# All cache pages by plain transfers of the SP queue, weight requests moved to ACT, no transfers on POOL

## The chip, the cores and the metric

The kernel runs on one core of one Trainium2 chip. The metric is the device time of one execution in microseconds; lower is better. The engines are named as the profile names them: PE is TensorE's matmuls, PEld its weight loads, DVE is VectorE, ACT is ScalarE, POOL is GpSimd and SP is SyncE. Each engine runs its own list of instructions in order. SP, ACT and POOL can also request DMA transfers; a request is an instruction in the list of the engine that makes it.

## The reference

Two layers of a decoder trunk run over 288 tokens: a prompt of 256 and 8 samples of 4 tokens each. Each layer is a half-step feed-forward block, a mixer and a second half-step feed-forward block:

```python
x = x + 0.5 * _swiglu(_rmsnorm(x, g_ffn1), w_up1, w_down1)
u, v, q, k, vv, qi, ki, wi, ga, gb = split(_rmsnorm(x, g_mix) @ w_in)
sv, attn = mixer(...)            # chunked spatial gating; sparse attention
x = x + (sigmoid(ga) * ((gelu(u) * sv) @ w_pa) + sigmoid(gb) * (attn @ w_pb)) @ w_out
x = x + 0.5 * _swiglu(_rmsnorm(x, g_ffn2), w_up2, w_down2)
# sample mixer: a paged cache of 2048 past positions for each of 8 samples
ki_all = concatenate([cache_kidx[page_table], ki])   # 16 pages of 128 positions a sample
_, idx = top_k(index_scores(qi, wi, ki_all), 256)
attn = sparse_attend(q, cache_k[phys, off], cache_v[phys, off], valid)
```

Model width is 1024, feed-forward width 2816, 8 heads of 128, 2 key heads. The page table is data: which page of the pool holds which positions is known only at run time. The kernel scores all keys and masks those outside the top 256, so each layer reads all 128 pages of the index cache, of the key cache and of the value cache.

## The kernel before, in words

All work on weights is a list of 420 units. A unit is a block of 128 output columns of a weight matrix, 128 x 8 x 128 numbers (512 KB; 448 KB in the second and third third of a down-projection). `unit_dma(i)` requests unit i from memory into one of four buffers `raw`. `unit_split(i)` cuts it into a high and a low part: ACT copies `wh` from `raw`, then DVE subtracts `wl` from `raw` and `wh`; each of the two has three buffers. `unit_mm` then runs 24 matmuls of 288 columns over them (21 for a short unit). In the main loop at the end of `trunk`, unit i's matmuls stand behind the split of unit i+2, and the split of unit i requests unit i+4, into the buffer that unit i has just left. That request is an instruction of SP and waits until DVE has made `wl` of unit i.

In program order each layer is FFN 1 (44 units up, 24 units down), the mixer (73 units) and FFN 2 (68 units). Between the units' matmuls stand the mixer's own, smaller ones; generators that the main loop calls in turn record them. The order of all instructions is fixed when the program is built. `Clocks` and `Engine.cost` keep a running estimate for each engine, and a generator stands back until its data are ready by that estimate.

`loader` brings in the cache pages in the order of `want`: for each layer four tiles of index pages (8 samples x 4 pages each), 16 tiles of keys and 16 tiles of values, each tile 1 MB. The first index tile goes to `kx`, all others to a ring of four buffers `ring`; a ring buffer is refilled once its reader on PE has used it (`drop_tile`). Index pages come by gathers that POOL requests, two pages of 32 KB in one gather: 16 gathers a tile. Of the key and value tiles, every other page of 128 KB comes by a gather of POOL, and the page between by SP: SP loads the page number into a register (`value_load`) and requests a plain transfer whose address the register gives. Row numbers for the gathers (`idxk`, `idxK`) are worked out on DVE in `late`. The index tiles of layer 0 load during FFN 1 of layer 0, those of layer 1 once the attention of layer 0 has ended, that is late in the mixer of layer 0; key and value tiles load during the mixers.

POOL does a little arithmetic besides: `rs` (the power -0.5 of a norm), some products in the mixer, and whatever `either` gives it. The paced loop in `loader` lets a page be recorded only while the estimate of POOL's and SP's clocks is at most `PRM["ahead"]`, 4 us, ahead of PE's.

Of the kernel before, what the change touches and what calls it, by code (L numbers as in the profile page):

```python
# [12 lines left out]
I32 = mybir.dt.int32  # L13
# [10 lines left out]
L = 2  # L24
# [86 lines left out]
class Clocks:  # L111
# [35 lines left out]

    def transfer(self, t, w):

        b = self.busy = [x for x in self.busy if x[1] > self.t["PE"] - 10000]  # L150
        i = 0
        while i < len(b) and b[i][0] < t + w:
            t = max(t, b[i][1])
            i += 1
        b.insert(i, (t, t + w))
        return t

    def slot(self, tensor):
# [41 lines left out]
class Engine:  # L200
# [3 lines left out]
        self.c, self.n, self.e, self.table, self.mode = clocks, name, engine, None, None  # L204

    def cost(self, k, a, kw):
        out = a[0] if a else kw["out"]
        if k in ("max", "match_replace"):
            out = a[1] if k == "max" else a[0]
        n = 1  # L210
        for d in out.shape[1:]:
            n *= d
        if self.n == "PE":
            lhs, z = a[1], 2 if a[1].dtype == F32 else 1
            rows, cols = lhs.shape[0], lhs.shape[-1]
            mode = ((128 if rows > 64 else 64 if rows > 32 else 32), 128 if cols > 64 else 32)
            turn = 0 if mode == self.mode else 95
            self.mode = mode
            n = 1
            for d in (a[2].shape if k == "matmul" else out.shape)[1:]:  # L220
                n *= d
            if k == "transpose":
                return turn + max(n * z / 2.4 + 2.5, 50)
            if lhs.dtype == F32R:
                return turn + max(0.4355 * n + 6, 60)
            w = z * max(n * z / 2.4 + 2.5, 109 if z == 2 else 54)
            if mode[1] == 32:
                w = z * max(n * z / 2.4 + 2.5, 54) / 4 * (1.45 if mode[0] == 64 else 1)
            return turn + w
        if self.n == "V":  # L230
            quick = k in ("tensor_copy", "memset", "tensor_scalar") and "accum_out" not in kw
            quick = quick and not (len(a) > 1 and str(getattr(a[1], "space", "")).endswith("PSUM"))
            w = 69 + n * (0.52 if quick else 6.5 if k == "reciprocal" else 1.04)
            for v in list(a[2:]) + [kw.get("scalar"), kw.get("scale")]:
                if hasattr(v, "ap") and v.shape[-1] == 1:
                    w += 61
            return w
        if self.n == "S":
            psum = str(getattr(a[1], "space", "")).endswith("PSUM")
            w = (51 if psum else 93) + 0.833 * n + 93 * ("accum_out" in kw)  # L240
            w += 94 * (hasattr(kw.get("scale"), "ap") + hasattr(kw.get("bias"), "ap"))
            t = self.TABLES.get(a[2])
            if t and t != self.table:
                self.table = t
                w += 1283
            return w
        if k == "indirect_dma_start":
            return 1250 if n > 128 else 1600
        if k == "dma_start":
            return 475  # L250
        if k == "value_load":
            return 585
        return 150 + (170 if kw.get("op") == OP.pow else 2.4) * n

    def __getattr__(self, k):
        f = getattr(self.e, k)

        def call(*a, **kw):
# [6 lines left out]
            outs = [] if k == "value_load" else outs  # L265
# [3 lines left out]
            if k in ("dma_start", "indirect_dma_start"):  # L269
# [4 lines left out]
                t0 = c.transfer(c.t[self.n] + (2000 if self.n == "Q" else 1000), size * 4 / 320.0)  # L274
                by, end = "DMA", t0 + size * 4 / 320.0 + 1800
# [17 lines left out]
def trunk(ctx, tc, A, OUT):  # L293
# [10 lines left out]
    rgp = ctx.enter_context(tc.tile_pool(name="rgp", bufs=4))  # L304
# [11 lines left out]
    pts = cp.tile([1, DB * PG], I32, name="pts")  # L316
    idxk = cp.tile([128, L, 4, PG], I32, name="idxk")
    idxK = cp.tile([128, L, DB, PG], I32, name="idxK")
# [145 lines left out]
    def unit_dma(i):  # L464
# [191 lines left out]
    def drop_tile(key):  # L656
        del tiles[key]
        state["used"] += key[0] != "i" or key[2] != 0

    def loader():  # L660
        yield from wait("idx")
        n = 0
        for key in want:
            kind, l = key[0], key[1]
            extra = kind == "i" and key[2] == 0
            if extra:
                yield from wait((l - 1, "attn") if l else "idx")
                t = mp.tile([128, LW], F32, tag="lg1", name="kx")[:, :2048]
            else:
                while n - state["used"] >= 4:  # L670
                    yield
                n += 1
                t = rgp.tile([128, 2048], F32, tag="ring", name="ring")
            if kind == "i":
                v = t.rearrange("p (j g s) -> p j g s", j=4, g=4)
                for j in range(4):
                    for g in range(4):
                        pg = g * 4 + key[2]
                        while clk["P"] > clk["PE"] + PRM["ahead"]:
                            yield  # L680
                        P.indirect_dma_start(
                            out=v[:, j, g], out_offset=None, in_=A["kidx"],
                            in_offset=bass.IndirectOffsetOnAxis(ap=idxk[:, l, j, pg:pg + 1], axis=0))
                        yield
            else:
                v = t.rearrange("p (b g f) -> p b g f", b=4, g=2)
                grp, pp = key[2], key[3]
                src = A["kT"] if kind == "k" else A["cv"]
                for b in range(4):
                    while max(clk["P"], clk["Q"]) > clk["PE"] + PRM["ahead"]:  # L690
                        yield
                    for g in range(2):
                        col = (grp * 4 + b) * PG + pp * 2 + g
# [9 lines left out]
                    yield  # L703
            tiles[key] = v


# [803 lines left out]
    def late():  # L1510
        Q.dma_start(cbf, A["cbf"])
        Q.dma_start(cct, A["cct"])
        Q.dma_start(pts, A["pt"].rearrange("a b -> (a b)")[None, :])
        ptb = mp.tile([128, DB, PG], I32, tag="lg0", name="ptb")
        pt = A["pt"]
        Q.dma_start(ptb, bass.AP(tensor=pt.tensor, offset=pt.offset, ap=[[0, 128], [1, DB * PG]]))
        yield from ready(ptb, on="V")
        pv = ptb.rearrange("p (j a) g -> p a j g", a=2)
        for l in range(L):
            V.tensor_scalar(idxK[:, l], ptb, 128.0, cst[:, O_P:O_P + 1], op0=OP.mult, op1=OP.add)  # L1520
            for par in range(2):
                hs = slice(64 * par, 64 * par + 64)
                V.tensor_scalar(idxk[hs, l], pv[hs, par], 64.0, cst[hs, O_P64:O_P64 + 1], op0=OP.mult, op1=OP.add)
            if l:
                V.tensor_scalar(idxK[:, l], idxK[:, l], float(l * POOL * 128), None, op0=OP.add)
                V.tensor_scalar(idxk[:, l], idxk[:, l], float(l * POOL * 64), None, op0=OP.add)
        flags.add("idx")

    spawn(late())
# [39 lines left out]
    spawn_front(rms_gen((0, 1)))  # L1569
    unit_dma(3)  # L1570
    unit_dma(4)
    unit_dma(5)

    pend = []

# [68 lines left out]
def _pack(inputs):  # L1644
# [24 lines left out]
    a["kidx"] = c(f["cache_kidx"].transpose(0, 1, 3, 2).reshape(L * POOL * 64, 128))  # L1669
    a["pt"] = c(f["page_table"])  # L1670
    a["cst"], a["cbf"], a["cct"] = _consts()
    return a

# [27 lines left out]
```

## Time and profile before

| what | value |
|---|---|
| median of 3 runs | 1839.77 us (1828.89 to 1846.6) |
| the profiled execution's own time | 1844.01 us |
| its span, first to last instruction | 1842.3 us |
| PE busy | 1612.0 us, 12110 matmuls |
| ACT busy | 756.2 us |
| POOL busy | 432.1 us |
| mean granted TensorE clock | 0.918 of full |

The profiled execution took 1.7 us more than its span. Busy times are those of the engines' own work; time in which an engine only issues a DMA or waits does not count on ACT, DVE or SP, while a gather of POOL counts as POOL's work. The stages of the program, read from when each unit's first matmul starts, are FFN 1 of layer 0 up to about 298 us, its mixer to 795 us, its FFN 2 to 1006 us, then layer 1 with FFN 1 to 1218 us, mixer to 1626 us and FFN 2 to the end.

### The profile page before, as it was taken

What the parts mean: (1) busy time and instruction counts of PE and PEld (TensorE: products, weight loads), DVE (VectorE), ACT (ScalarE), POOL (GpSimd) and SP (SyncE); (2) the same over time, 40 slices, a digit from 0 to 9 for tenths busy, and PEclk for the clock granted to TensorE, in tenths of its full rate; (3) what the DMA queues carried; (4) which work ended last, traced back from release to release, by engine and by line L of the source; (5) the groups of instructions that cost most, each with busy time, mean ns of one, the idle gap of its engine ahead of it and who ended that gap; (6) DMA issues with size and microseconds to landing.
All of it is one profiled execution on the core that took longest, in us unless ns stands there. A gap on an engine that the chain in (4) does not pass through costs nothing.

```text
span 1842.3 us, 32306 instructions
## 1 busy us (share of the span) xinstructions
PE 1612.0 (87%) x12110; PEld 1504.3 (82%) x12110; DVE 983.8 (53%) x2013; ACT 756.2 (41%) x1227; POOL 432.1 (23%) x435
## 2 busy tenths in 40 slices
PE   8249999888878716999999999999878889999999
PEld 7249999677656615999999999997666678999999
DVE  6026656665624202666655666568545344666653
ACT  4014444343545202454444444445335653454432
POOL 4730001243645572010000000012545540000000
PEclk9569999887979856999999999999889989999999
DMA  6225554456665523455455454544565655544453
GB/s 234 74 90 162 176 167 148 134 168 202 188 196 168 186 63 98 163 183 169 163 165 167 159 168 159 168 146 158 184 207 178 215 164 194 170 157 166 165 166 120
DMA packets 121742, 299.80 MB, mean 163 GB/s; under 512 B 19826, under 2 KB 57331, under 8 KB 121587
## 3 DMA queue, kind: packets, MB, share of 16 engines
q1 hardware_dynamic: 105202, 255.77, 43.1%
q0 software_dynamic: 16384, 41.97, 7.5%
q8 instruction: 96, 1.57, 0.3%
q14 instruction: 60, 0.48, 0.1%
HBM read 294.90 MB, written 2.77 MB: 162 GB/s over the span
## 4 chain that ended last, share of the span: by engine, by line
PE 76%; issue 17%; another core or an unknown queue 2%; DVE 2%; POOL 2%; DMA 1%; ACT 0%; SPq 0%; POOLq 0%; DVEq 0%; ACTq 0%
PE mm L282 66%; PE s L282 10%; POOL ring L282 1%; DVE b L282 0%; DVE jk L282 0%; POOL rs L282 0%; DVE wl L282 0%; ACT b L282 0%; DMA x<-in_x 0%; SPq L282 0%; DMA ring<-in_kT,idxK 0%; DMA ring<-in_cv 0%; DVE ci L282 0%; ACT wh L282 0%
## 5 line engine op out<-in xcount | busy, mean ns | idle before, releaser
L282 PE MATMUL mm<-b,wh 128*128 128x288 f32 x6560 | 1376.7, 304 | 101.4 <-issue 98.2
L282 PEld LDWEIGHTS mm<-b,wh 128*128 128x128 f32 x6560 | 1083.4, 193 | 142.5 <-issue 136.4
L282 PE MATMUL mm<-b,wl 128*128 128x288 f32 x3280 | 986.5, 301 | 55.0 <-issue 54.1
L282 ACT ACTIVATE wh<-raw 128x1024 fp32r<-128x1024 f32 (+3 forms) x421 | 435.6, 1035 | 690.5 <-issue 351.0
L282 PEld LDWEIGHTS mm<-b,wl 128*128 128x128 f32 x3280 | 634.9, 194 | 57.7 <-issue 56.5
L282 DVE TENSOR_TENSOR wl<-raw,wh 128x1024 fp32r<-128x1024 f32 (+3 forms) x421 | 503.9, 1197 | 322.7 <-ACT wh L282 271.1
L282 POOL TENSOR_TENSOR rs<-ms,mhalf 128x3 f32<-128x3 f32 x8 | 11.6, 1448 | 822.4 <-DVE ms L282 822.4
L282 POOL DMA_INDIRECT ring<-in_kT,idxK x128 | 127.7, 997 | 129.8 <-PE s L282 96.2
L282 POOL DMA_INDIRECT ring<-in_cv,idxK x128 | 129.3, 1010 | 119.2 <-PE s L282 50.5
L282 POOL DMA_INDIRECT ring<-in_kidx,idxk x96 | 92.4, 963 | 29.2 <-issue 28.6
L282 DVE TENSOR_TENSOR tc<-mm,tb 128x288 f32<-128x288 f32 x88 | 40.3, 458 | 107.1 <-remote 60.6
L282 DVE TENSOR_TENSOR ta<-mm,rb 128x288 f32<-128x288 f32 x88 | 40.3, 458 | 68.4 <-PE mm L282 45.0
L282 ACT ACT_TABLE_LOAD x44 | 56.5, 1283 | 8.5 <-PE s L282 5.3
L282 ACT ACTIVATE b<-s 128x16 fp32r<-128x16 f32 (+2 forms) x66 | 18.0, 286 | 84.7 <-PE s L282 38.8
L282 ACT ACTIVATE jk<-z,ci 128x513 bf16<-128x513 f32 x32 | 23.2, 725 | 69.3 <-DVE ci L282 63.8
L282 PE MATMUL s<-ring,b 128*32 128x256 f32 x512 | 43.7, 433 | 4.3 <-issue 3.8
L282 DVE TENSOR_SCALAR_CACHE_REDUCE jk<-z,ci 128x513 bf16<-128x513 f32 x60 | 45.1, 752 | 2.2
L282 ACT ACTIVATE ta<-mm 128x288 f32<-128x288 f32 x32 | 13.1, 409 | 72.4 <-issue 47.2
L282 DVE TENSOR_TENSOR tb<-ta,rb 128x288 f32<-128x288 f32 x88 | 39.8, 452 | 3.3 <-ACT ta L282 3.3
L282 ACT ACTIVATE b<-tc 128x288 fp32r<-128x288 f32 x88 | 37.7, 428 | 5.0 <-issue 4.4
L282 DVE TENSOR_TENSOR b<-tc,b 128x288 fp32r<-128x288 f32 x88 | 39.7, 451 | 0.0
L282 POOL DMA_INDIRECT kx<-in_kidx,idxk x32 | 33.8, 1056 | 23.1 <-issue 9.1
(201 smaller groups left out, 975.6 us busy)
## 6 DMA issues: line engine op xcount, KB each, us to landing
raw<-in_wup SPq DMA_DIRECT2D x175, 512.0 KB
raw<-in_win SPq DMA_DIRECT2D x96, 512.0 KB
raw<-in_wdn SPq DMA_DIRECT2D x64, 448.0 KB
ring<-in_kT SPq DMA_DIRECT2D x128, 128.0 KB
raw<-in_wdn SPq DMA_DIRECT2D x32, 512.0 KB
ring<-in_cv SPq DMA_DIRECT2D x128, 128.0 KB
raw<-in_wpa SPq DMA_DIRECT2D x16, 512.0 KB
raw<-in_wpb SPq DMA_DIRECT2D x16, 512.0 KB
```

What stands on the lines that cost most here:

```text
L282: r = f(*a, **kw)
```

## The change

All pages now come by plain transfers that SP requests, and POOL requests none. `pages` loads four page numbers into four registers with one load, and four transfers follow. The address's range check before each transfer is left to the transfer. An index page is a transfer of its own (32 KB to 64 partitions), so an index tile takes 32 of them instead of 16 gathers. The page table comes in an order that suits the groups of four, and `idxk`, `idxK` and the DVE work that made them are gone. From unit 3 on, ACT requests the weight units; the split of unit i requests unit i+3 instead of i+4, so that the buffer asked for is that of unit i-1. The loader starts when PE's estimate reaches 40 us. The estimates change with it (520 ns a request, 700 ns a register load, a transfer that may be cut into pieces between others), three more small blocks are free for the mixer, and POOL's scratch memory for gathers is smaller.

```diff
-NB = 64
+NB = 67
+RING = 4
...
     def cost(self, k, a, kw):
+        if k == "dma_start":
+            return 520
...
-        if k == "indirect_dma_start":
-            return 1250 if n > 128 else 1600
-        if k == "dma_start":
-            return 475
-        if k == "value_load":
-            return 585
...
-            Q.dma_start(v, u["src"])
+            (S if i > 2 else Q).dma_start(v, u["src"])
...
         if i > 1:
-            unit_dma(i + 4)
+            unit_dma(i + 3)
...
+    def pages(c):
+
+        clk["Q"] += 700
+        return nc.values_load_multi_w_load_instructions(
+            pts[0:1, c:c + 4], engines=[mybir.EngineType.SP], min_val=0, max_val=POOL - 1,
+            skip_runtime_bounds_check_because="each transfer checks its address against the cache's bounds")[1]
+
+    def turn():
+        while clk["Q"] > clk["PE"] + PRM["ahead"]:
+            yield
...
             if kind == "i":
                 v = t.rearrange("p (j g s) -> p j g s", j=4, g=4)
                 for j in range(4):
-                    for g in range(4):
-                        pg = g * 4 + key[2]
-                        while clk["P"] > clk["PE"] + PRM["ahead"]:
-                            yield
-                        P.indirect_dma_start(
-                            out=v[:, j, g], out_offset=None, in_=A["kidx"],
-                            in_offset=bass.IndirectOffsetOnAxis(ap=idxk[:, l, j, pg:pg + 1], axis=0))
-                        yield
+                    for par in range(2):
+                        yield from turn()
+                        for g, rv in enumerate(pages(DB * PG + 32 * key[2] + 8 * j + 4 * par)):
+                            Q.dma_start(v[64 * par:64 * par + 64, j, g],
+                                        A["kidx"][l][bass.ds(rv, 1)].rearrange("a p f -> p (a f)"))
...
-                        if g == 0:
-                            P.indirect_dma_start(
-                                out=v[:, b, g], out_offset=None,
-                                in_=src.rearrange("l a p f -> (l a p) f"),
-                                in_offset=bass.IndirectOffsetOnAxis(
-                                    ap=idxK[:, l, grp * 4 + b, pp * 2 + g:pp * 2 + g + 1], axis=0))
-                        else:
-                            rv = Q.value_load(pts[0:1, col:col + 1], min_val=0, max_val=POOL - 1)
-                            Q.dma_start(v[:, b, g], src[l][bass.ds(rv, 1)].rearrange("a p f -> p (a f)"))
-                    yield
+                for b in range(0, 4, 2):
+                    yield from turn()
+                    for i, rv in enumerate(pages(64 * grp + 8 * pp + 2 * b)):
+                        Q.dma_start(v[:, b + i // 2, i % 2], src[l][bass.ds(rv, 1)].rearrange("a p f -> p (a f)"))
...
-        yield from ready(ptb, on="V")
...
+        Q.dma_start(pts, A["pt"])
+        while clk["PE"] < 40000:
+            yield
         flags.add("idx")
```

The order of the instructions shows three places. On POOL, from the first norm of FFN 1 of layer 0 to the start of its mixer, the list before is this (`kx` and `ring` are page tiles, `in_kidx` and `in_kT` the index and the key cache, `b` a block of the mixer):

```order
L282 TENSOR_TENSOR accp<-accp,sq 128x288
L282 TENSOR_TENSOR rs<-ms,mhalf 128x3
L282 DMA kx<-in_kidx,idxk 128x128 x16
L282 DMA ring<-in_kidx,idxk 128x128 x48
L282 DMA ring<-in_kT,idxK 128x256 x4
L282 TENSOR_TENSOR rs<-ms,mhalf 128x3
L282 TENSOR_TENSOR b_2805<-x,rb 128x288
```

The same stretch of POOL's list now:

```order
L294 TENSOR_TENSOR sq<-x 128x288
L294 TENSOR_TENSOR accp<-accp,sq 128x288
L294 TENSOR_TENSOR rs<-ms,mhalf 128x3 x2
L294 TENSOR_TENSOR b_3125<-x,rb 128x288
L294 TENSOR_TENSOR b_3131<-x,rb 128x288
```

The 68 gathers are gone from between the two norms, and nothing takes their place on POOL.

On SP, among the key tiles of the mixer of layer 0, before (in brackets the semaphores that a row waits for; the DMAs of SP and of ACT go round eight of them, `DMAHW0` to `DMAHW7`, and each waits for the last transfer of its own):

```order
L282 DMA ring<-in_kT 128x256 [waits DMAHW4_49]
L282 DMA raw<-in_win 128x1024 [waits DMAHW5_49,DVE_49]
L282 TENSOR_LOAD pts
L282 ISA x3
L282 DMA ring<-in_kT 128x256 [waits DMAHW6_49]
```

The same tiles on SP now:

```order
L673 TENSOR_LOAD pts
L294 ISA
L294 DMA ring<-in_kT 128x256 [waits DMAHW3_49,PE_49]
L294 ISA
L294 DMA ring<-in_kT 128x256 [waits DMAHW4_49]
L294 ISA
L294 DMA ring<-in_kT 128x256 [waits DMAHW5_49]
L294 ISA
L294 DMA ring<-in_kT 128x256 [waits DMAHW7_49]
```

One register load now serves four pages, one register operation stands before a transfer where there were three a page, and the weight requests have left SP.

On ACT, early in FFN 1 of layer 0, before:

```order
L282 ACTIVATE wh<-raw 128x1024 [waits DMAHW4_49,PE_49,Activation_49]
L282 ACTIVATE b_456<-tc 128x288 [waits DVE_49]
L282 ACTIVATE wh<-raw 128x1024 [waits DMAHW5_49,PE_49,Activation_49]
L282 ACTIVATE ta<-ta 128x288 [waits DVE_49,Activation_49]
L282 ACTIVATE wh<-raw 128x1024 [waits DMAHW6_49,PE_49,Activation_49]
```

The same stretch of ACT's list now:

```order
L294 ACTIVATE wh<-raw 128x1024 [waits DMAHW5_49,PE_49]
L294 DMA raw<-in_wup 128x1024 [waits DMAHW4_49,DVE_49]
L294 ACTIVATE b_357<-tc 128x288 [waits DVE_49]
L294 ACTIVATE wh<-raw 128x1024 [waits DMAHW2_49,PE_49]
L294 DMA raw<-in_wup 128x1024 [waits DMAHW1_49,DVE_49]
L294 ACTIVATE ta<-ta 128x288 [waits DVE_49,Pool_49]
```

Behind each `wh` now stands a weight request that waits for DVE and for an earlier transfer of the same semaphore, whichever engine asked for that one.

## Rows read from the trace of the kernel before

**Rows 1.** The page: busy time of engines (part 1), and 40 slices (part 2).
```profile
PE 1612.0 (87%) x12110; PEld 1504.3 (82%) x12110; DVE 983.8 (53%) x2013; ACT 756.2 (41%) x1227; POOL 432.1 (23%) x435
...
PE   8249999888878716999999999999878889999999
...
POOL 4730001243645572010000000012545540000000
PEclk9569999887979856999999999999889989999999
```
**Rows 2.** Busy time by stretches: stretch, length, five engines with instructions, clock, DMA share, GB/s.
```profile
22.00:302.00 280.00, 220.10 (x1564) 215.16 (x1564) 126.56 (x186) 91.84 (x129) 67.20 (x68) 0.86 0.45 141
302.00:640.00 338.00, 278.40 (x2182) 230.72 (x2181) 177.21 (x550) 149.40 (x288) 153.62 (x155) 0.88 0.56 176
640.00:804.00 164.00, 108.41 (x711) 103.37 (x712) 60.14 (x93) 44.72 (x68) 54.35 (x56) 0.76 0.36 117
804.00:1011.00 207.00, 207.00 (x1568) 206.98 (x1568) 125.69 (x180) 91.98 (x129) 1.35 (x3) 1.00 0.53 168
1011.00:1223.00 212.00, 211.57 (x1600) 211.23 (x1599) 126.98 (x181) 91.30 (x129) 1.86 (x2) 1.00 0.52 163
1223.00:1562.00 339.00, 292.60 (x2336) 247.62 (x2335) 188.93 (x568) 158.78 (x305) 144.49 (x142) 0.91 0.57 182
```
**Rows 3.** What ended PE's waits, 804 to 1223 us: total us, times, longest.
```profile
PE s L282 <- POOL rs L282: 0.4, 1, 0.4
```
**Rows 4.** The order of time, 108 to 111 us: start, length, engine, idle before.
```profile
108.45 0.94 POOL L282 DMA_INDIRECT ring<-in_kidx,idxk  x1 [0.30 <-issue]
109.23 0.28 PEld L282 LDWEIGHTS mm<-b,wl 128*128 128x128 f32 x1 [2.52 <-issue]
109.70 0.94 POOL L282 DMA_INDIRECT ring<-in_kT,idxK  x1 [0.30 <-issue]
110.63 0.40 PE L282 MATMUL mm<-b,wl 128*128 128x288 f32 x1 [2.40 <-issue]
```
**Rows 5.** What ended PE's waits, 302 to 640 us.
```profile
PE mm L282 <- issue: 21.1, 33, 2.7
PE s L282 <- issue: 14.4, 19, 1.5
```
**Rows 6.** What ended PE's waits, 1223 to 1562 us.
```profile
PE s L282 <- issue: 20.0, 20, 6.1
PE mm L282 <- issue: 16.6, 27, 1.1
```
**Rows 7.** Groups of instructions by operation: busy us, mean ns of one, idle before.
```profile
L282 ACT ACTIVATE wh<-raw 128x1024 fp32r<-128x1024 f32 (+3 forms) x421 | 435.6, 1035 | 690.5 <-issue 351.0 <-PE mm L282 221.5 <-remote 100.4
L282 POOL DMA_INDIRECT ring<-in_cv,idxK x128 | 129.3, 1010 | 119.2 <-PE s L282 50.5 <-issue 32.6 <-DMA ring<-in_cv 23.6
L282 POOL DMA_INDIRECT ring<-in_kidx,idxk x96 | 92.4, 963 | 29.2 <-issue 28.6 <-DMA ring<-in_kidx,idxk 0.6
L282 ACT ACT_TABLE_LOAD x44 | 56.5, 1283 | 8.5 <-PE s L282 5.3 <-PE mm L282 1.9 <-PEq L1680 0.7
```
**Rows 8.** SP's requests in the order of time, at the start and in the first mixer.
```profile
1.65 1.85 SPq L282 DMA_DIRECT2D raw<-in_wup  x4
...
390.37 13.02 SPq L282 DMA_DIRECT2D ring<-in_kT  x7
...
411.38 3.73 SPq L282 DMA_DIRECT2D ring<-in_kT  x4
```
**Rows 9.** ACT's groups, 804 to 1011 us.
```profile
L282 ACT ACTIVATE wh<-raw 128x1024 fp32r<-128x1024 f32 (+1 forms) x67 | 69.4, 1036 | 113.7 <-issue 83.5 <-PE mm L282 30.2
```

More of the change, by code (lines that the diff above doesn't have):

```diff
@@ L148, in transfer @@
     def transfer(self, t, w):
[L150 to L153, printed above, removed]
+        b = [x for x in self.busy if x[1] > self.t["PE"] - 10000]
+        out, i = [], 0
+        while i < len(b) and b[i][1] <= t:
+            out.append(b[i])
             i += 1
-        b.insert(i, (t, t + w))
+        while w > 0.01:
+            if i < len(b) and b[i][0] <= t:
+                t = max(t, b[i][1])
+                out.append(b[i])
+                i += 1
+                continue
+            e = min(t + w, b[i][0] if i < len(b) else t + w)
+            w -= e - t
+            out.append((t, e))
+            t = e
+        merged = []
+        for x in sorted(out + b[i:]):
+            if merged and x[0] <= merged[-1][1] + 1e-6:
+                merged[-1] = (merged[-1][0], max(merged[-1][1], x[1]))
+            else:
+                merged.append(x)
+        self.busy = merged
         return t
@@ L264, in call @@
                 outs.append(a[0])
-            outs = [] if k == "value_load" else outs
             ins = [v for v in aps if not any(v is o for o in outs)]
@@ L268, in call @@
             why = c.why
-            if k in ("dma_start", "indirect_dma_start"):
+            if k == "dma_start":
                 size = 1
@@ L273, in call @@
                 c.t[self.n] = max(c.t[self.n], dep) + w
-                t0 = c.transfer(c.t[self.n] + (2000 if self.n == "Q" else 1000), size * 4 / 320.0)
-                by, end = "DMA", t0 + size * 4 / 320.0 + 1800
+                t0 = c.t[self.n] + 2000
+                by, end = "DMA", c.transfer(t0, size * 4 / 320.0) + 1800
             else:
@@ L303, in trunk @@
     hlp = ctx.enter_context(tc.tile_pool(name="hlp", bufs=3))
-    rgp = ctx.enter_context(tc.tile_pool(name="rgp", bufs=4))
+    rgp = ctx.enter_context(tc.tile_pool(name="rgp", bufs=RING))
     tp = ctx.enter_context(tc.tile_pool(name="tp", bufs=2))
@@ L315, in trunk @@
     gns = cp.tile([128, L, NG], F32, name="gns")
-    pts = cp.tile([1, DB * PG], I32, name="pts")
-    idxk = cp.tile([128, L, 4, PG], I32, name="idxk")
-    idxK = cp.tile([128, L, DB, PG], I32, name="idxK")
+    pts = cp.tile([1, 2 * DB * PG], I32, name="pts")
     mhalf = cp.tile([128, 1], F32, name="mhalf")
@@ L664, in loader @@
             kind, l = key[0], key[1]
-            extra = kind == "i" and key[2] == 0
-            if extra:
+            if kind == "i" and key[2] == 0:
                 yield from wait((l - 1, "attn") if l else "idx")
@@ L669, in loader @@
             else:
-                while n - state["used"] >= 4:
+                while n - state["used"] >= RING:
                     yield
@@ L688, in loader @@
                 src = A["kT"] if kind == "k" else A["cv"]
-                for b in range(4):
-                    while max(clk["P"], clk["Q"]) > clk["PE"] + PRM["ahead"]:
-                        yield
-                    for g in range(2):
-                        col = (grp * 4 + b) * PG + pp * 2 + g
-                        if g == 0:
-                            P.indirect_dma_start(
-                                out=v[:, b, g], out_offset=None,
-                                in_=src.rearrange("l a p f -> (l a p) f"),
-                                in_offset=bass.IndirectOffsetOnAxis(
-                                    ap=idxK[:, l, grp * 4 + b, pp * 2 + g:pp * 2 + g + 1], axis=0))
-                        else:
-                            rv = Q.value_load(pts[0:1, col:col + 1], min_val=0, max_val=POOL - 1)
-                            Q.dma_start(v[:, b, g], src[l][bass.ds(rv, 1)].rearrange("a p f -> p (a f)"))
-                    yield
+                for b in range(0, 4, 2):
+                    yield from turn()
+                    for i, rv in enumerate(pages(64 * grp + 8 * pp + 2 * b)):
+                        Q.dma_start(v[:, b + i // 2, i % 2], src[l][bass.ds(rv, 1)].rearrange("a p f -> p (a f)"))
             tiles[key] = v
@@ L1512, in late @@
         Q.dma_start(cct, A["cct"])
[L1513 to L1516, printed above, removed]
-        yield from ready(ptb, on="V")
[L1518 to L1526, printed above, removed]
+        Q.dma_start(pts, A["pt"])
+        while clk["PE"] < 40000:
+            yield
         flags.add("idx")
@@ L1668, in _pack @@
     a["cv"] = c(f["cache_v"].reshape(L, POOL, 128, 256))
-    a["kidx"] = c(f["cache_kidx"].transpose(0, 1, 3, 2).reshape(L * POOL * 64, 128))
-    a["pt"] = c(f["page_table"])
+    a["kidx"] = c(f["cache_kidx"].transpose(0, 1, 3, 2).reshape(L, POOL, 64, 128))
+    pt = f["page_table"]
+    a["pt"] = c(np.concatenate([pt.reshape(2, 4, 8, 2).transpose(0, 2, 1, 3).reshape(1, -1),
+                                pt.reshape(4, 2, 4, 4).transpose(3, 0, 1, 2).reshape(1, -1)], 1))
     a["cst"], a["cbf"], a["cct"] = _consts()
```

3 lines of the change are left out of this document (1 added, 2 removed).

## The prediction

> **What bounds the kernel now.** The page comes first. PE is busy for 1612 of 1842 us, so PE's time is what counts, and the slices show where it is missing [rows 1]. PE drops to 1 to 4 tenths in the second and third slice (46 to 138 us) and to 1 in the fifteenth (644 to 690 us), in the middle of stages that are nothing but weight matmuls. In the same slices POOL stands at 7, 3 and 7, and the clock falls to about half, while in the long rows of 9 POOL is at 0. Next, the stretches give the price of clean work [rows 2]: from 804 to 1011 us PE does 1568 matmuls in 207 us at full clock, 0.132 us each, with no idle time and three POOL instructions.
>
> Then the waits say what PE waited for. In the clean stretch it is nothing worth telling [rows 3]. In the bad ones the cause reads "issue": PE waited for nothing that the trace shows. The order of time shows what that looks like [rows 4]. POOL starts one gather of index pages after another, 1.25 us from start to start, and PE, with a full buffer of weights in front of it, runs one instruction in 1.4 us: a load at 109.23, its matmul at 110.63. Gathers and such waits go together through the whole trace: stretches with gathers have them, in both layers and for both sizes of page [rows 5, 6], and the clean FFN stages have none [rows 3], although weights stream there at 168 GB/s [rows 2]. That is a coincidence in time and not yet a cause.
>
> The mixers are bound by PE too, less cleanly: from 302 to 640 us it is busy for 278.4 of 338 us at a clock of 0.88, from 1223 to 1562 us for 292.6 of 339 us at 0.91 [rows 2]. The largest cause of idle time is again "issue": 21.1 + 14.4 us and 20.0 + 16.6 us [rows 5, 6].
>
> **The change part by part.** The sum is made against the profiled execution's 1844.0 us (span 1842.3), which lies 4 us above the median of the three runs, so the same stalls are in those runs.
>
> 1. The gathers of index pages go. Layer 0: the stretch 22 to 302 us has 1564 matmuls, at 0.132 us 206.5 us; it took 280 us, so **73.5 us** are lost. Layer 1's index tiles load at the end of the first mixer: the stretch 640 to 804 us has 711 matmuls, 93.9 us of work in 164 us, **70.1 us** lost [rows 2]. I take both back in full, because behind the stall nothing else is late: DVE and ACT follow PE there and idle longer than it does. Sum 143.6 us. If plain transfers disturb PE in the same way, nothing of this comes back; that is a rival.
>
> 2. The gathers of key and value pages go, 256 of about 1.0 us [rows 7]. PE's gaps by "issue" in the mixers add up to 72.1 us [rows 5, 6]. Clocks of 0.88 and 0.91 mean 24% and 18% of the stretch at the lower of the clock's two levels, 1.2 instead of 2.4 GHz; at PE's busy share of 0.82 and 0.86 that is 66 and 53 us of cold work, of which at most half, 59 us, would be given back. The bounds are thus 0 and 131 us. I take two thirds of the gaps, since behind some of them PE would meet a wait for DVE or ACT, and a quarter of the clock: 48 + 15 = **63 us**.
>
> 3. SP takes all pages. A bare request is 1.85 / 4 = 0.46 us; a page before, with its own load and three register operations, (3.73 - 0.46) / 3 = 1.09 us when undisturbed [rows 8]. With one load for four pages and one operation a page, the price lies between 0.46 + 0.63 / 4 = 0.62 and 1.09 us; I take 0.7, near the lower end because most of the 0.63 us is what goes. A key or value tile is then 5.6 us of SP; before it was four gathers, 4 x 1.25 = 5.0 us, beside four pages of SP, 4.4 us. 256 pages are 179 us of a mixer stretch of 338 us, so the pages fit. The index tiles, 128 transfers a layer, take 90 us instead of 80, beside FFN work that does not need them for another 100 us: no cost.
>
> 4. ACT takes 418 weight requests at 0.46 us. In FFN it is busy for 92 of 207 us and idles 113.7 us ahead of its 67 `wh` [rows 2, 9]; 67 x 0.46 = 31 us fit into that. In the mixers it is 73 x 0.46 = 34 us, and five more table loads of 1.28 us [rows 7], on 149 of 338 us busy. Little of PE's waiting is put to ACT there; I take 5 us a mixer, **10 us**, bounds 0 and 40 us (the whole of it in one mixer).
>
> 5. The waits that the change adds. A weight request now stands in ACT's list, and behind it the evacuations of PE's results and the next `wh`. It waits for DVE's `wl` of unit i-1, which lies a unit, 24 x 0.132 = 3.2 us, back: nothing. It also waits for the transfer that used its semaphore last, eight DMAs before it in the program, and among pages that is one of SP's. So ACT is held when SP falls behind the order in which pages and weights were written down, which counts 0.52 + 0.70 / 4 = 0.695 us a page. At 0.7 us SP keeps pace: I take 5 us a layer for single waits, **10 us**. At 1.09 us it falls behind by 0.395 x 128 = 51 us in each layer's index tiles, and ACT, and PE after it, with it.
>
> 6. Weights are asked for one unit later, three units ahead of their split, 9.5 us. No `wh` of the clean stretch waited for a transfer [rows 9]; 512 KB at the 317 GB/s that 168 GB/s at a share of 0.53 come to [rows 2] are 1.7 us. Cost nothing; the cover is the two units that lie split ahead of PE. The eight small DVE instructions of `late`, the three blocks more and the smaller scratch change nothing that PE waits for. Requests of units 3 and 4 come later at the start, behind ACT's squares, but their matmuls are two units away: nothing.
>
> Sum: 1844.0 - 73.5 - 70.1 - 63 + 10 + 10 = 1657 us, against the median 4 less: **1653 us**.
>
> A rule of the Trainium skill speaks against the largest terms. The page "DMA: Bandwidth & Descriptors", section "Issuing engines are not separate DMA queues", says that transfers from SP, ACT and POOL run on the same 16 DMA engines and that another issuing engine only saves the sequencer's time to start them. By that rule the sum would stay at the time before, since POOL's time was on nobody's path; the trace does not bear it out for POOL's gathers, beside which PE runs one instruction in 1.4 us with the DMA share of the stretch at 0.45 [rows 2, 4].
>
> **The rivals.**
>
> *The page price.* SP needs 1.09 us a page also in groups of four, because the register operations and not the load are the cost, and ACT is held behind it at the shared semaphores: + 101 us, 1653 + 101 = 1754 us. For it: no row splits the 0.63 us. Against it: two of three operations and three of four loads are gone.
>
> *The stalls belong to the pages, not to POOL.* PE gaps come with short rows landing in scattered order, whoever requests them. Then the stalls and the mixers' gaps stay and the queues alone change: about 1840 us. For it: in the mixers SP's pages and POOL's gathers always run together, so the trace does not separate them there. Against it: in the stalls of the second, third and fifteenth slice [rows 1] the pages are index pages, which POOL alone requests; the first key page of POOL's list comes at 109.70 us [rows 4].
>
> *Slower: SP is disturbed by its own register loads.* Among gathers a page of SP took (13.02 - 0.46) / 6 = 2.09 us [rows 8]. If that disturbance comes from loading addresses and stays, SP is now alone with all pages: 128 x (2.09 - 0.695) = 179 us a layer during which ACT and PE wait in FFN, and 256 x 2.09 = 535 us of pages in a mixer stretch of 339, 196 us more. In all 1653 + 2 x (179 + 196) = 2403 us. It decides from about 1.37 us a page on: there 2 x 128 x 0.675 + 2 x (351 - 339) = 197 us eat up the gain of 187. Against it: at 411 us four pages went at 1.09 us in the same stretch.
>
> **How the numbers follow.** The forecast, 1600 to 1735 us, has 0.80. Its low end is item 2 near its upper bound (1653 - 53, of at most 68 more); its high end is item 2 at nothing with half the ACT bound (1653 + 63 + 20 = 1736). Under 1600 us: 0.05. The page price, 1735 to 1821 us: 0.07. Pages and not POOL, or the queue alone: 0.04. Slower: 0.04. The range of the forecast holds 8 in 10 and is taken as it is. One per cent is about what a measurement of this kernel can tell from no change; the three runs before lie within 1%. So faster 0.92, the same 0.04, slower 0.04.
>
> **What would show it.** Right: PE at 9 in all slices of FFN 1 of layer 0 and of the end of the first mixer, with 207 to 215 us for an FFN; no PE wait by "issue" of any size; the mixers' stretches shorter by some 30 us each, at a clock above 0.92; POOL busy for about 50 us. The page price is read from SP's requests in the order of time: four pages within 2.8 us. Wrong: gaps by "issue" beside SP's pages, 0.7 us ticks on SP itself; ACT's `wh` or evacuations waiting for transfers named `ring` or `kx`; a clean FFN but a mixer as long as before, which would say that the gaps there hid waits for DVE and ACT.

## The result and the profile after

The changed kernel takes **1547.0 us** (median of 4 runs, 1545.2 to 1547.7) against 1839.1 us: ratio 0.8413, 95% interval 0.8372 to 0.8455. It is faster, as forecast, but by 292 us where 187 were forecast; the time lies below the range (1600 to 1735).

The page of the changed kernel, busy time and slices, answers to [rows 1]:

```profile
PE 1515.0 (98%) x12110; PEld 1444.6 (93%) x12110; DVE 976.0 (63%) x1987; ACT 768.6 (50%) x1241; POOL 52.5 (3%) x65
...
PE   8999999999999999999999999999999999999999
...
POOL 1000011100000000000000000201000000000000
PEclk9999999999999999999999999999999999999999
```

PE stands at 9 from the second slice on, and the clock does not fall in any slice. Its busy time fell by 97 us for the same 12110 matmuls.

Busy time of the changed kernel by stretches (columns as in [rows 2]): FFN 1 of layer 0, a clean FFN 2, then the two mixers.

```profile
5.00:221.00 216.00, 212.30 (x1596) 210.67 (x1595) 135.99 (x195) 98.93 (x144) 5.46 (x7) 0.99 0.65 204
566.00:779.00 213.00, 212.59 (x1604) 212.34 (x1603) 127.80 (x183) 93.17 (x131) 1.77 (x1) 1.00 0.54 172
221.00:516.00 295.00, 282.95 (x2481) 250.19 (x2481) 194.19 (x570) 173.16 (x323) 20.34 (x25) 0.99 0.72 226
991.00:1281.00 290.00, 280.96 (x2478) 248.21 (x2476) 194.10 (x570) 172.93 (x324) 20.39 (x25) 1.00 0.71 224
```

Stages are counted here, and everywhere below, from their first weight matmul to that of the next stage, and "mixer" means its first 57 units: its last 16 (51 us in both kernels) count as a stage of their own. So counted, FFN 1 of layer 0 went from 292.3 to 216.0 us, the mixers from 446.5 and 357.4 to 294.3 and 289.8; no other stage moved by more than 2 us.

What PE still waits for in the first mixer, 221 to 516 us, answers to [rows 5]:

```profile
PE s L294 <- DMA ring<-in_kT: 3.1, 3, 2.4
PE s L294 <- DVE b L294: 2.6, 1, 2.6
PE s L294 <- DMA ring<-in_cv: 1.7, 1, 1.7
```

"Issue" is gone, and nothing that it could have hidden took its place: the largest releaser is worth 3.1 us in all. SP's requests in the order of time (compare [rows 8]), and ACT's most numerous one in the list of DMA issues (KB, us to landing):

```profile
29.04 12.45 SPq L294 DMA_DIRECT2D kx<-in_kidx  x16
42.02 20.14 SPq L294 DMA_DIRECT2D ring<-in_kidx  x26
252.49 16.79 SPq L294 DMA_DIRECT2D ring<-in_kT  x24
```
```profile
raw<-in_wup ACTq DMA_DIRECT2D x173, 512.0 KB, 3.5
```

A page costs SP 0.78 us in the index tiles (12.45 us for 16) and 0.70 us in the mixers (16.79 us for 24).

### The profile page after: what moved, and what is told of

The parts are those of the page before. It is cut to its first block, busy times and chain, and to the rows that moved or that the text cites. A ratio compares the mean times of both kernels' runs of the same rounds, so it can differ in the third digit from the quotient of the medians.

```text
span 1545.8 us, 32344 instructions
## 1 busy us (share of the span) xinstructions
PE 1515.0 (98%) x12110; PEld 1444.6 (93%) x12110; DVE 976.0 (63%) x1987; ACT 768.6 (50%) x1241; POOL 52.5 (3%) x65
## 4 chain that ended last, share of the span: by engine, by line
PE 77%; issue 14%; DMA 4%; ACT 2%; DVE 2%; SPq 1%; POOL 1%; POOLq 0%; DVEq 0%; ACTq 0%
PE mm L294 71%; PE s L294 6%; DMA raw<-in_win 1%; DMA ring<-in_kT 1%; DMA ring<-in_cv 1%; SPq L294 1%; ACT L294 1%; POOL rs L294 0%; DVE b L294 0%; DVE wl L294 0%; ACT b L294 0%; ACT wh L294 0%; DMA b<-in_ws 0%; DMA x<-in_x 0%; ACT lg L294 0%
## 5 line engine op out<-in xcount | busy, mean ns | idle before, releaser
L294 PE MATMUL mm<-b,wh 128*128 128x288 f32 x6560 | 1327.5, 298 | 4.8 <-DVE b L294 2.6
L294 PEld LDWEIGHTS mm<-b,wh 128*128 128x128 f32 x6560 | 1047.5, 188 | 24.4 <-issue 14.3
L294 PE MATMUL mm<-b,wl 128*128 128x288 f32 x3280 | 965.9, 294 | 2.3 <-DVE wl L294 1.6
L294 PEld LDWEIGHTS mm<-b,wl 128*128 128x128 f32 x3280 | 615.9, 188 | 3.5 <-DVE wl L294 3.5
L294 PE MATMUL s<-ring,qz 128*32 128x256 f32 x512 | 34.2, 383 | 4.4 <-DMA ring<-in_kT 4.4
L294 ACT ACTIVATE ta<-ta 128x288 f32<-128x288 f32 x88 | 37.8, 430 | 0.8 <-DVE ta L294 0.7
L294 PE MATMUL s<-ring,b 128*32 128x256 f32 x512 | 33.9, 382 | 2.5 <-DMA ring<-in_cv 2.5
L294 DVE SCALAR_TENSOR_TENSOR x<-mm,x 128x288 f32<-128x288 f32 x32 | 14.7, 458 | 31.4 <-PE mm L294 31.4
L294 PEld LDWEIGHTS s<-ring,qz 128*32 128x32 f32 x512 | 16.4, 109 | 16.5 <-issue 5.8
L294 PEld LDWEIGHTS s<-ring,b 128*32 128x32 f32 x512 | 16.7, 109 | 15.2 <-DMA ring<-in_cv 5.3
```

The lines of the kernel that those rows point to most:

```text
L294: r = f(*a, **kw)
```

## The experiments

Each run stands beside runs of the kernel before on the same chip, and these turned out to matter most: on three chips (and in the runs of the result) the kernel before took 1837 to 1840 us, on three others 1518 to 1520 us. They are called **stalling** and **quiet** chips here. Each chip was used in one batch of runs only, so what belongs to the chip and what to the time of the batch was not separated. Each experiment is read beside the kernel before on its own chip.

### One part at a time, on a stalling chip (kernel before 1839.6 us)

**e1_index_pool**: the changed kernel, index pages as gathers again (with them come their row numbers on DVE, four small blocks fewer and the larger scratch memory).

```
-  for g, rv in enumerate(pages(...)): Q.dma_start(v[64*par:...], A["kidx"][l][bass.ds(rv, 1)]...)
+  P.indirect_dma_start(out=v[:, j, g], ..., in_offset=IndirectOffsetOnAxis(ap=idxk[:, l, j, pg:pg+1], axis=0))
```


> The changed kernel, with the index pages alone requested as gathers by POOL again (64 gathers a layer; key and value pages stay with SP, weight requests with ACT). Theory (POOL's gathers hold up the instruction lists of all engines while they run): the two long stalls come back and nothing else, 1547 + 144 = about 1690 us; the first FFN takes some 290 us again, the first mixer 70 to 80 us more than 345, the second mixer stays at 341 us. Rival (short rows of pages disturb PE whoever requests them, and the gain came from something else): 1547 us, since the same rows land. Rival (the gain came from taking weight requests out of SP's queue): 1547 us.

Measured 1623.3 us (ratio 0.882). The mixer of layer 0, at whose end layer 1's index pages load, took 365.2 us, so that stall was back. FFN 1 of layer 0 took 216.6 us: the same 64 gathers, no stall. Neither theory said that.

**e2_index_sp**: the kernel before, index pages by SP.

```
-                        P.indirect_dma_start(out=v[:, j, g], out_offset=None, in_=A["kidx"], ...)
+                        for g, rv in enumerate(pages(32 * key[2] + 8 * j + 4 * par)):
+                            Q.dma_start(v[64 * par:64 * par + 64, j, g], A["kidx"][l][bass.ds(rv, 1)]...)
```

> The kernel before, with the index pages alone requested by SP, four page numbers a load (key and value pages stay half POOL, half SP, weight requests stay on SP). Theory (POOL's gathers): the two stalls go, the mixers stay as they were, 1839 - 144 = about 1695 us. Rival (short rows): about 1839 us. Rival (weight requests in SP's queue): slower than 1839 us, since 256 more transfers stand ahead of the weights on SP.

1732.1 us (0.942). The stalls of FFN 1 and of the first mixer's end are gone (233.9 and 365.2 us), the mixers' own stay (368.0 us in layer 1). Beside the index pages SP now serves the weights late: FFN 1 of layer 0 is 17 us and the two stages behind that mixer are 22 us longer than in the kernel before on a quiet chip (e11 below).

**e3_weights_act**: the kernel before, weight requests on ACT.

```
-            Q.dma_start(v, u["src"])
+            (S if i > 2 else Q).dma_start(v, u["src"])
...
-            unit_dma(i + 4)
+            unit_dma(i + 3)
```


> The kernel before, with the weight requests alone moved to ACT, three units ahead. Theory (POOL's gathers): within 1% of 1839 us, since the gathers stay. Rival (weight requests in SP's queue): a good part of the 292 us comes back, under 1750 us.

The four runs took 1781, 1786, 1824 and 1864 us; even the shortest is outside the 1% that its theory allowed. Only the one of 1781 us left a trace: it has no stall in FFN 1 of layer 0 (217.5 us) and all the others (449.1 and 367.4 us in the mixers). That the longer executions had that stall too is likely by its size (75 us) and not shown. But POOL's gathers are those of the kernel before, which stalled there: the gather as such is not the price.

**e4_weights_sp**: the changed kernel with the weights back on SP.

```
-            (S if i > 2 else Q).dma_start(v, u["src"])
+            Q.dma_start(v, u["src"])
...
-            unit_dma(i + 3)
+            unit_dma(i + 4)
```

> The changed kernel, with the weight requests moved back to SP, four units ahead, so that SP requests everything. Theory (POOL's gathers): no stall returns; the requests of weights now stand behind 0.7 us a page on SP, so 1547 to 1570 us, what is lost lies in the mixers. Rival (weight requests in SP's queue): most of the gain goes, over 1700 us.

1550.5 us (0.8445), 3.5 us above the changed kernel. By the stages of the two profiled executions that near-zero is two larger terms: beside the index pages ACT's requests save 14.6 + 4.1 + 9.3 us (FFN 1 of layer 0 and the two stages behind its mixer), in the mixers they cost 15.2 and 10.8 us (279.1 and 279.0 us with SP). SP's requests also go out a unit earlier here; queue and lead were not tried apart.

### What a stall needs: gathers added where nothing else happens

FFN 1 of layer 1 is clean in the changed kernel (212.0 us). The next kernels add 64 gathers there, of 128 rows of 512 bytes each, into a tile that nobody reads.

```
+        for n in range(64):
+            P.indirect_dma_start(out=v[:, n % 16], out_offset=None, in_=rows, in_offset=...)
```

The first batch fell on a quiet chip (kernel before 1518.2 us):

> The changed kernel with 64 gathers of the pool back to back added in FFN 1 of layer 1 (212.0 us there), each of 128 rows of 512 bytes into a tile that nobody reads. Each gather costs about 1.1 us: that stage 280 us, in all 1617 us. Only when VectorE is quiet do they run at full rate and hold the others up, and VectorE works 60% there: 212 to 216 us, in all 1547 to 1552 us, or 1617 us in those executions in which it falls over.

1548.0 us, that stage 211.5 us. **e6_idle_plain**, with plain transfers of the pool:

```
+            P.dma_start(v[:, n % 16], rows[128 * (n % 16):128 * (n % 16) + 128])
```

> The same as the run with 64 added gathers, with plain transfers of the pool of the same rows in place of the gathers. If the pool's own work of writing a transfer's list disturbs the others, as the gathers do: as that run. If it is the gather alone: 1547 to 1552 us.

1548.2 us, 211.5 us. Two zeros on a chip on which the kernel before does not stall either; plain transfers of the pool were not tried on a stalling one. **e9_index_paced** puts an operation of the pool between the gathers of e1:

```
+                        if l == 1:
+                            P.tensor_tensor(pace, x[:, 0], x[:, 1], op=OP.mult)
```

> The index pages again as 128 gathers of the pool, key and value pages by SP, weights by ACT, as in the run that took 1623 us; the 64 gathers of layer 1 now have one elementwise operation of the pool between any two (288 elements a partition, into a tile that nobody reads), so that they can't follow each other at 1.25 us. Theory that each gather costs the other engines about 1.1 us, however they are spaced: the end of layer 0's mixer stays at 365 us, in all about 1623 us. Theory that only gathers that follow each other at their full rate hold the engines up: that mixer goes back to 294 to 300 us, in all 1550 to 1560 us. Rival, that it is the bytes of the pages in those 80 us: 1623 us too.

1585.8 us on the first quiet chip, and the same idea in the idle stage, on another quiet chip:

> The changed kernel with 64 gathers added in FFN 1 of layer 1, one elementwise operation of the pool between any two: nothing, 1545 to 1552 us, on either chip by the theory that only gathers at full rate cost; 1617 us if each costs 1.1 us on a chip where the kernel before takes 1839 us.

1572.2 us. Both were ill made. What DVE waited for in e9_index_paced, 500 to 810 us, and what DVE and then PE waited for in e7_idle_paced, 780 to 970 us:

```profile
DVE x L296 <- POOL pace L296: 23.1, 2, 19.4
```
```profile
DVE x L296 <- POOL spare L296: 28.3, 1, 28.3
```
```profile
PE mm L296 <- DVE wl L296: 23.1, 1, 23.1
```

The added operation reads `x`, DVE writes `x` later, and so DVE stood behind the pool's whole list: a wait by data that the edit put there. Both runs say nothing on pacing.

The kernels once more, unchanged, on that second quiet chip:

> The kernel before, unchanged, once more with its trace: in the last runs it took 1518 us beside 1839 us in those ahead of them, on another chip. If the stalls under the pool's gathers depend on the chip, its trace shows at 1518 us the same gathers with FFN 1 of layer 0 at about 215 us and the mixers at 275 to 285 us, and at 1839 us the known ones (292.3, 446.5, 357.4). If something else made up for them at 1518 us, the stalls are still there.

The kernel before takes 1519.5 us there. Its page:

```profile
PE 1500.4 (99%) x12110; PEld 1437.4 (95%) x12110; DVE 984.1 (65%) x2013; ACT 754.0 (50%) x1227; POOL 464.9 (31%) x435
...
PE   8999999999999999999999999999999999999999
...
POOL 4883004277777750000000000133777500000000
PEclk9999999999999999999999999999999999999999
...
L282 POOL DMA_INDIRECT ring<-in_kidx,idxk x96 | 116.3, 1212 | 29.3 <-issue 28.3
```

The same instructions and the same 384 gathers, POOL at 8 in the second and third slice, and PE at 9 beside it. A gather of index pages lasts 1212 ns here and 963 ns in [rows 7]: where the others work, the gathers are the slower ones.

> The changed kernel, unchanged, beside it: without gathers it should take 1545 to 1550 us on any chip. If the chip as a whole is faster: under 1530 us.

1551.1 us, ratio 1.0204 (1.0130 to 1.0279): on this chip the change makes the kernel **slower**, by about 2%.

> The changed kernel with the index pages as gathers of the pool, which took 1623 us where the kernel before took 1839 us. Where the kernel before takes 1518 us: no stall, 1547 to 1555 us, if the chip decides; 1580 to 1625 us if the order of the work decides. Where it takes 1839 us: 1618 to 1625 us again.

1552.1 us: no stall. The stretch in which e1's second burst ran on the stalling chip, then that of this run (columns as in [rows 2]):

```profile
440.00:560.00 120.00, 59.92 (x390) 49.09 (x383) 25.00 (x60) 27.43 (x61) 64.14 (x64) 0.69 0.42 134
```
```profile
440.00:570.00 130.00, 124.52 (x965) 119.48 (x956) 75.45 (x134) 64.61 (x114) 72.84 (x64) 0.96 0.69 225
```

64 gathers in both; they take POOL 64 us where PE stands and 73 us where PE works.

The new theory: work beside them keeps the gathers apart; if VectorE falls quiet, they follow each other at full rate, and on a stalling chip the others then get their instructions one by one until the burst ends. So a pause was made in the middle of the burst, by copies on ACT behind which the units' `wh` come late:

```
+            if n == 20:
+                for m in range(28):
+                    S.e.activation(t[:, 1536:2048], cst[:, :512], AF.Copy)
```

> The changed kernel with 64 gathers of the pool added in FFN 1 of layer 1 (212 us without them), and ahead of the 21st of them 28 copies on ACT (512 elements a partition, constants, into a part of a tile that nobody reads), some 15 us, so that the units' copies come late and TensorE and VectorE have nothing to do for some 8 us in the middle of the burst. Theory that a quiet VectorE lets the gathers go to their full rate and that this state then holds itself to the end of the burst: about 8 + 43 x 1.2 = 60 us more than without either, FFN 1 of layer 1 at 265 to 275 us, on any chip. Rival, that the stall comes from outside the kernel, of the chip: where the kernel before takes 1518 us, only the 8 us, 220 us; where it takes 1839 us, 270 to 290 us.

The pause alone has `pass` in place of the gather.

> The same 28 copies on ACT and no gathers: what the pause alone costs, 5 to 12 us, FFN 1 of layer 1 at 217 to 224 us by both theories.

On a stalling chip (1836.9 us) the stage took 276.1 us with both, 225.9 us with the pause alone; totals 1611.5 and 1563.7 us. Then without and with the pause on one chip, again a stalling one (1838.8 us):

> The 64 added gathers in FFN 1 of layer 1 without a pause, which cost nothing (211.5 us there) on a chip where the kernel before takes 1518 us. Where it takes 1837 us, as on the chip of the run with the pause: if the pause started the stall, 212 to 216 us; if such a chip stalls by itself, 260 to 290 us. Where it takes 1518 us: 212 us again.

> The same gathers with the pause of some 14 us ahead of the 21st. If a quiet VectorE is all that it takes, the stall follows the pause on every chip: 265 to 280 us. If it is the chip: 276 us again where the kernel before takes 1837 us, and 226 us, the pause alone, where it takes 1518 us.

Without it 211.5 us (1551.9 in all), with it 276.2 us (1613.5). And with the pause on a quiet chip (1518.7 us):

> The gathers with the pause once more. If the kernel before takes 1518 us beside it: 265 to 280 us in FFN 1 of layer 1 if the pause starts a stall on any chip, 226 us (the pause alone) if such a chip doesn't stall. If it takes 1837 us: 276 us for the third time, and the question of the other chips stays open.

225.6 us, just the pause (1564.8 in all). The 60 us from 825 us on, the last 4 us of the pause and what follows it, in four kernels. Gathers without a pause, stalling chip:

```profile
825.00:885.00 60.00, 60.00 (x456) 60.00 (x455) 38.98 (x57) 26.41 (x38) 48.53 (x38) 1.00 0.59 207
```

Gathers with the pause, the same chip:

```profile
825.00:885.00 60.00, 26.21 (x101) 20.22 (x102) 9.43 (x14) 10.46 (x16) 46.28 (x46) 0.59 0.31 102
```

Gathers with the pause, quiet chip, and the pause alone, stalling chip:

```profile
825.00:885.00 60.00, 53.93 (x391) 53.58 (x392) 36.66 (x54) 30.25 (x45) 48.42 (x39) 0.91 0.60 208
```
```profile
825.00:885.00 60.00, 55.77 (x403) 55.42 (x404) 37.90 (x56) 29.17 (x43) 0.00 (x0) 0.92 0.49 170
```

PE runs 456, 101, 391 and 403 matmuls. In this stage only pause, gathers and a stalling chip together give the stall. (With the pause the gathers write 12 slots of the tile and not 16, on both kinds of chip.) In the order of time it looks as it did in [rows 4]; with the pause on the stalling chip:

```profile
858.22 0.95 POOL L296 DMA_INDIRECT spare<-in_kidx,idx  x1 [0.30 <-issue]
858.25 0.29 PEld L296 LDWEIGHTS mm<-b,wh 128*128 128x128 f32 x1 [0.20 <-issue]
859.47 0.94 POOL L296 DMA_INDIRECT spare<-in_kidx,idx  x1 [0.30 <-issue]
859.65 0.40 PE L296 MATMUL mm<-b,wh 128*128 128x288 f32 x1 [1.25 <-issue]
860.36 0.29 PEld L296 LDWEIGHTS mm<-b,wh 128*128 128x128 f32 x1 [1.83 <-issue]
```

and on the quiet chip, at the same place:

```profile
856.79 1.23 DVE L296 TENSOR_TENSOR wl<-raw,wh 128x1024 fp32r<-128x1024 f32 x1 [0.50 <-ACT wh L296]
857.22 1.61 POOL L296 DMA_INDIRECT spare<-in_kidx,idx  x1 [0.30 <-issue]
```

On the one chip gathers of 0.94 us start 1.25 us apart and PE's next matmul starts 1.40 us after its load; on the other a gather that meets a `wl` lasts 1.61 us, and PE goes on.

The pause starts the stall, but not in the way of the theory. e18_push_again, stalling chip, then the same `ta` on the quiet chip (e19_push_third):

```profile
810.05 18.50 ACT L1542 ACTIVATE spare<-cst 128x512 f32<-128x512 f32 x28
829.53 1.23 DVE L296 TENSOR_TENSOR wl<-raw,wh 128x1024 fp32r<-128x1024 f32 x1 [17.01 <-ACT spare L1542]
834.60 0.45 DVE L296 TENSOR_TENSOR b<-tc,b 128x288 fp32r<-128x288 f32 x1
839.15 0.46 DVE L296 TENSOR_TENSOR ta<-mm,rb 128x288 f32<-128x288 f32 x1 [4.10 <-PE mm L296]
840.56 0.38 PE L296 MATMUL mm<-b,wh 128*128 128x288 f32 x1 [0.27 <-issue]
```
```profile
836.80 0.46 DVE L296 TENSOR_TENSOR ta<-mm,rb 128x288 f32<-128x288 f32 x1 [0.64 <-PE mm L296]
```

In the pause the gathers run at full rate and ACT's 28 copies are not held up: they take 18.50 us on either chip. Behind it VectorE works from 829.5 to 835 us without a gap. Only then does it stand for 4.10 us, while PE works on without a wait until 840 us. And in FFN 1 of layer 0 of the kernel before no pause comes ahead of the stall at all: from 27 to 40 us VectorE never idles for more than 1.0 us at a time, and PE works without a wait until 43.8 us.

```profile
39.75 0.50 DVE L282 TENSOR_TENSOR tb<-ta,rb 128x288 f32<-128x288 f32 x1
43.54 0.29 PE L282 MATMUL mm<-b,wl 128*128 128x288 f32 x1
44.58 0.43 PE L282 MATMUL mm<-b,wh 128*128 128x288 f32 x2 [0.74 <-issue]
46.73 0.46 DVE L282 TENSOR_TENSOR tc<-mm,tb 128x288 f32<-128x288 f32 x1 [6.49 <-remote]
```

So neither a quiet VectorE nor a quiet TensorE is what a stall needs; a pause can bring one on, and what sets it off otherwise is open.

### A version that is faster than the changed kernel

By e4's stages the weights belong on ACT beside the index pages and on SP in the mixers:

```
+    def on_sp(i):
+        return 68 <= i % 209 < 125
...
-            (S if i > 2 else Q).dma_start(v, u["src"])
+            (S if i > 2 and not on_sp(i) else Q).dma_start(v, u["src"])
...
-            unit_dma(i + 3)
+            while nxt[0] <= i + 3 + on_sp(nxt[0]):
+                unit_dma(nxt[0])
+                nxt[0] += 1
```


> The changed kernel with the weight requests of the two mixers' 57 units each on SP again, four units ahead, the others on ACT. By the stages of the run with all weights on SP (mixers 279.1 and 279.0 us against 294.3 and 289.8) and of the changed kernel (the other stages): 1547 - 26 = 1521 us. If the mixers' gain needs the weights of the stages around them on SP as well: about 1547 us.

1526.9 us on a quiet chip, ratio 1.0060 (1.0043 to 1.0077).

> The kernel with the mixers' weights on SP and the others on ACT, once more, with an interval: 1522 to 1530 us on any chip, since it has no gathers; against the kernel before 1.003 to 1.008 where that takes 1518 us, 0.83 where it takes 1839 us.

1526.2 us on a stalling chip, 0.8318 (0.8288 to 0.8348). Its mixers take 280.8 and 280.2 us. It is 21 to 24 us below the changed kernel on either kind (1547.0 and 1551.1 us, not side by side), below the kernel before on stalling chips, and 0.6% above it on quiet ones.

## Why the prediction was wrong

The runs split the fall into the steps of the forecast. Stalls removed: from the kernel before on a stalling chip (span 1842.3 us) to the same kernel on a quiet one (1517.7 us). The changed queues: from there to the changed kernel on the same quiet chip (1545.2 us).

- **Item 1, index gathers, 73.5 + 70.1 us.** FFN 1 of layer 0: 292.3 - 216.8 = 75.5 us. Layer 1's burst: e1 on a stalling less on a quiet chip, 365.2 - 297.1 = 68.1 us. Sum 143.6 us, as forecast; each part is 2 us off, and that the two cancel to the tenth is luck.
- **Item 2, key and value gathers, 63 us of at most 131: this step failed.** The mixers of the kernel before lose (446.5 - 277.4) + (357.4 - 277.4) = 249.1 us to stalls; less layer 1's burst, 181.0 us. That the gathers of key and value pages are the reason was also seen on one stalling chip: layer 1's mixer took 367.4 us with them and 294.9 us without when ACT requested the weights (e3, e1), 368.0 and 279.0 us when SP did (e2, e4).
- **Items 3 to 6, the new requests, 10 + 10 us.** 1545.2 - 1517.7 = 27.5 us on one chip. They sit in the mixers (+10.4 and +14.9 us); putting the weights there on SP again gave back 20 us. The page price was right for the mixers (0.70 us taken).

Sum: -143.6 - 181.0 + 27.5 = -297.1 us; the profiled executions differ by 1844.0 - 1547.6 = 296.4 us.

Item 2's error lies in both of its parts. Layer 1's mixer in the kernel before, on the stalling chip and then on the quiet one:

```profile
1218.00:1576.00 358.00, 311.60 (x2480) 266.52 (x2479) 197.81 (x579) 166.70 (x316) 144.63 (x142) 0.92 0.57 181
```
```profile
974.00:1251.00 277.00, 273.18 (x2473) 244.34 (x2472) 197.08 (x579) 165.49 (x315) 144.78 (x142) 1.00 0.71 234
```

PE's idle time falls from 46.4 us (36.6 of it by "issue" [rows 6]) to 3.8 us and its busy time from 311.6 to 273.2 us. "Two thirds of the gaps" was wrong, since nothing stood behind them: late dispatch had also made DVE's and ACT's results late, and these waits went with it. "A quarter of the clock" was wrong, since the clock had fallen only because of the gaps, and all of it came back. The bound of 131 us failed as well, since it counted only waits named "issue", and cold work by the clock alone: a clock of 0.92 means 57 us at the lower level and explains at most 29 of the 38 us by which the busy time fell. What the other 9 to 10 us were is not settled; nor is it settled how much of layer 0's excess (101 us, bound 68) was idle time and how much clock. Slips in the working that changed nothing: the second and third slice read 2 and 4 tenths and not 1 to 4, and the fifteenth lies in the first mixer; the program has 418 units and not 420, and ACT requests 415 of them; the high end of the range counts 20 us for ACT on top of the 10 us in the sum.

**The rivals.** The page price fell with 0.70 to 0.78 us a page. "The stalls belong to the pages" fell with e1 and e2: index pages by SP stall nothing, by gathers they do at the end of the first mixer. "Slower" did not come on stalling chips; on quiet ones the change is slower by about 2%, but by the weight requests in the mixers and not by SP's register loads, since its pages go at 0.70 us there. As for the Trainium skill's rule ("DMA: Bandwidth & Descriptors", "Issuing engines are not separate DMA queues"), by which another issuing engine only saves sequencer time: on quiet chips the runs agree that nothing else is gained, though about 2% is lost; on stalling ones they do not, with 292 us. But the change also turned gathers into plain transfers, and of that the rule does not speak.

**The mechanism.** The argument "gathers and issue waits go together" was right for the trace and incomplete as a cause. It needs a stalling chip, and there a pause in the burst brings the stall on where it does not come by itself; in FFN 1 of layer 0 the kernel before stalled without a pause, and e1 and e3 did not stall. What sets a stall off, why the gathers of a stalling chip hold up the dispatch, and what differs between the chips, was not found; all six ran the same program. That the result was measured on a stalling chip, like the rows, was luck for the forecast "faster": nothing in it allowed for a chip on which the change costs 2%.

## What to carry to other kernels

A wait that reads "issue" on all engines at once, beside one engine that runs at its full rate, was one state here and not many gaps: when its cause went, nearly all idle time and all cold work in it went too, so count both whole and not by shares. Before a tuned kernel is changed, run it unchanged on a second chip: this one's "defect" of 320 us was absent on three of six, and there the cure costs 2%. Put each stream of requests on the queue that has time in that stage; a sum over the program hid a gain of 28 us and a loss of 26 us.

## What was not expected of the hardware

- The same program takes 1837 to 1840 us on some chips and 1518 to 1520 us on others, each within 1% in repeated runs (one batch a chip), and programs without gathers take the same on both (the mixed version 1526.2 and 1526.9 us).
- A stall under gathers outlasts what starts it: it set in some 6 us behind a pause that cost 14 us, and lasted to the end of the burst, some 50 us on.
- A gather of the pool that overlaps a `wl` of VectorE is slower: 1.17 us on average over 223 of them against 0.96 us for the other 161 (e11's trace), single ones 1.6 us. Where gathers are slowed so, the others work undisturbed.
- A weight request took ACT's queue 0.33 to 0.37 us, yet 57 of them cost layer 1's mixer some 10 us: PE's busy time there was 281.0 us with them and 276.6 us without, at the same full clock.
